# Layer 1's stick-breaking values and keys by two 1024-column units in a leading ordered list

## The chip, the cores and the metric

The kernel runs on one core of one Trainium2 chip. The metric is the device time of one execution in microseconds (us). The kernel before has a median of 2146.02 us over three runs (2145.95 to 2146.85). The core has five engines that matter here: PE (TensorE, the matmuls), DVE (VectorE), ACT (ScalarE), POOL (GpSimd) and SP (SyncE, which issues the loads). Each takes its instructions in the order in which the program wrote them.

## The reference

Two layers, each a hybrid of two kinds of attention beside each other, an output projection, and an MLP, all in float32 on x of 256 rows by 2048 columns:

```
for l in range(2):
    h = rms_norm(x, attn_norm)
    proj = h @ w_in                       # 2048 x 6160
    g_q, g_k, g_v, g_gate, g_lr, s_q, s_k, s_v = split(proj)
    o_gla = gla_chunked(g_q, g_k, g_v, log_sigmoid(g_lr @ w_gate_up + b_gate) / 16)
    o_gla = rms_norm(o_gla) * silu(g_gate)
    o_sb  = rms_norm(stick_breaking(rms_norm(s_q), rms_norm(s_k), s_v))
    x = x + concat(o_gla, o_sb) @ w_o
    x = x + square(relu(rms_norm(x) @ w_up)) @ w_down     # 8192 hidden
```

The columns of `proj` that this change touches are s_v (stick-breaking values, 1024 columns), s_k (keys, 1024 columns) and the first 512 columns of g_v (GLA values, 1024 columns) of the first layer.

## The kernel before, in words

**Precision.** Every large matmul is done as three: each float32 operand is split in a high part (rounded to the matmul's own format by an ACT copy, `whi`) and a low part (the remainder, a DVE subtraction, `wlo`), and the products high x high, high x low and low x high are summed in PSUM. A raw weight tile is loaded by SP, ACT writes its `whi`, DVE its `wlo`, PE reads both. For some tiles the low part is made without DVE: ACT writes the negated high part and a DMA issued by POOL adds the raw weights to it (`dlo`).

**Two kinds of code.** The attention part of a layer is written as *plain units*: `unit` computes all 256 rows by up to 512 columns from all 2048 inputs in four groups of weights, two halves each, 12 matmuls of 512 columns per half, 96 in all (L577, L578, L579). Small work between the units is hung on ticks by `after(n, fn)`: it is issued n halves later. The rest of a layer (second half of the gate, output projection, MLP) is one *ordered list*: every step is entered in a `Plan` with an engine, a length and its dependences, PE, SP and POOL keep the order in which steps were entered, and for DVE and ACT the planner writes an order by due times, by playing the list through with its own lengths. The list starts with five PE pieces of 12 matmuls each that stand for the end of the plain unit before it.

**Units of the list.** A unit of 1024 columns takes its 2048 inputs in eight pairs of 128-row blocks. A pair is a 2 x 2 block product for rows and inputs, so eight products of three matmuls (24 matmuls of 512 columns). For the pairs in `FAST = (1, 3, 5, 6)` it is done with seven products (21 matmuls), Strassen's scheme: DVE first makes sums of the weights (`first` and two `vector` steps, L1092) and of the activations (`forms`: `sums` with four 128x128 subtractions, L436 to L439, `high` on ACT, L450, and `low` on DVE, L454). The pairs in `ADDED = (2, 7)` have their low parts by the POOL DMA (L1269, L1272). The units called `iv` and `ik` are s_v and s_k of the *next* layer, done so at the end of a layer's list. Their results are scaled by the row norms (`AF.Copy` with `st["rst"]`, L1464) and kept in `natural`.

**Order of the first layer.** x is loaded in four parts (xb), PE turns each (L469) and ACT and DVE make the high and low operand `hT` from it (L479, L485). The first plain unit, s_v columns 0 to 511, starts on the first part while the others arrive by hooks after its halves. The row norms `st["rst"]` need the sums of squares of all x: `norm_squares` on ACT (L511), hung on ticks 6 to 9, then `norm_finish`. After it: s_k 0 to 511, the unit of the gate's low-rank and first query columns (272 wide), 256 query columns, s_v 512 to 1023, s_k 512 to 1023, s_q, four transposed units for g_q and g_k, g_v 0 to 511, g_v 512 to 1023, the first half of the gate; then the layer's ordered list. The second layer has the same attention part without the four s_v and s_k units, which the first layer's list has done.

**Pools.** The attention's temporaries lie in a scope `att`, the list's in a scope `mlp`, which take each other's place in SBUF; PSUM is cut into two accumulators and four small tiles for the attention, and into eight single banks for a list. Activations rotate through 17 buffers (`act`).

Of the kernel before, what the change touches and what calls it, by code (L numbers as in the profile page):

```python
# [144 lines left out]
def trunk_kernel(  # L145
# [60 lines left out]
    ATT = ("wg", "ident16", "mask16", "tri", "nones", "gmask", "reset", "v4", "lr", "lrT", "ha", "hh", "hl", "hA", "on", "dec", "S", "kdz", "row", "bc")  # L206
# [24 lines left out]
    open_scope("sbuf", att=1)  # L231
# [99 lines left out]
    def load_small():  # L331
        load_gains(1, (
            ("sq", sb_q_norm, 1), ("sk", sb_k_norm, 1), ("mlp", mlp_norm, KT),
            ("gla", gla_out_norm, 1), ("so", sb_out_norm, 1),
        ))
        load_gate_up(0)
# [85 lines left out]
    def forms(op, i, t, tag):  # L422
# [35 lines left out]
    def operand_parts(op, n, h2, key, l, place):  # L458
# [30 lines left out]
        def scaled():  # L489
            t = tmp("t2", [P, 2, T], bufs=T2)  # L490
# [6 lines left out]
    def norm_operand(op, n, key, l, sums=False):  # L497
        for h2 in range(2):
            turn, high, low, scaled = operand_parts(op, n, h2, key, l, ps_tile)
            turn()  # L500
            if sums and fast(2 * n + h2):
                for part in forms(op, 2 * n + h2, scaled(), "sxh"):
                    part()
            else:
                high()
                low()
# [288 lines left out]
    hT = Operand()  # L795
    ssq = new_ssq()
    st = {}
    his = []
    load_gains(0, (("attn", attn_norm, KT),))
    load_x(0, parts=2)  # L800
    wait_on_x(WARM0)
    st["first"] = turn_gains(0)
    norm_operand(hT, 0, "attn", 0)
    wait_on_x(WARM1)

    for l in range(DEPTH):
        wl = w_in[l]
        mixed = Operand()
        nxt = {}

        if l == 0:
            hooks = {}

            def next_x(n):
                load_x(n)
                with tc.issue_after(st["mm"]):
                    norm_operand(hT, n, "attn", 0)

            for n, at in ((1, (0, 0)), (2, (0, 1)), (3, (1, 1))):
                hooks[at] = lambda n=n: next_x(n)  # L820

            def begin():
                st["rst"] = norm_finish(ssq)

            for n in range(4):
                after(6 + n, lambda n=n: norm_squares(n, ssq))
            after(10, begin)
            after(2, build_constants)
            after(7, load_small)
            after(11, finish_small)  # L830
            uv = unit(
                hT, wl, 0, C_SV, 512, hooks=hooks, fine=1,
                order=lambda i, k: his[4 * i + (3 if i else k)] if i or k else None,
            )
            v = tmp("v4", [P, NT, 512], bufs=2)
            after(3, lambda a=uv, b=v: values(a, b))
        else:
            open_scope("sbuf", att=1)
            att_psum()
            load_gate_up(l)  # L840
            after(2, build_constants)
            v = natural["iv"][0]

        def sb_heads(g, qT, kT, v, first):

            state = {}

            def scores(hp):
                state[hp] = sb_scores(qT, kT, 2 * hp)
                after(3, lambda: weights(hp))  # L850

            def weights(hp):
                state[hp] = sb_weights(*state[hp])
                after(1, lambda: outs(hp))

            def outs(hp):
                po = ps_tile()
                for j in range(2):
                    sb_out(po, j, state[hp], v, 2 * hp + j)
                o = norm_pair(po)  # L860
                after(3, lambda: to_operand(mixed, 4 + 2 * g + hp, o, gain("so", l)))

            for hp in range(2):
                after(first[hp], lambda hp=hp: scores(hp))


        if l == 0:
            uk = unit(hT, wl, 0, C_SK, 512)
            rst = st["rst"]
            kT = act_tile(F32)  # L870
            sb_qk(uk, 0, 4, 0, rst, None, kT, 4)
        else:
            rst = st["rst"]
            kT = act_tile(F32)
            sb_qk(None, 0, 4, 0, rst, None, kT, 3, natural["ik"][0])
        ua = unit(hT, wl, 0, C_LR, RANK + 2 * P)
        lr = tmp("lr", [P, NT, RANK], bufs=1)
        for tt in range(NT):
            nc.vector.tensor_scalar(
                lr[:, tt, :], ua[:, tt, :RANK], rst[:, tt : tt + 1], None, ALU.mult  # L880
            )
        qT = act_tile(F32)
        sb_qk(ua, RANK, 2, 0, rst, gqk[:, l : l + 1], qT, 5)


        gt = {}

        def gate_rows():
            lrT = tmp("lrT", [RANK + 1, T], bufs=1)
            nc.gpsimd.memset(lrT, 1.0)  # L890
            plr = ps_tile()
            for tt in range(NT):
                nc.tensor.transpose(plr[:RANK, tt * P : (tt + 1) * P], lr[:, tt, :], ident)
            nc.vector.tensor_copy(lrT[:RANK, :], plr[:RANK, :T])
            gt["row"] = row_of(rst)
            gt["lrT"] = lrT

        def gates(b):
            if b == 0:
                gt["e"] = [act_tile(F32) for _ in range(3)]  # L900
                gt["dec"] = tmp("dec", [P, 4, 4], bufs=1)
            eb, enb, ekd = gt["e"]
            pl = ps_tile()
            for e in range(2):
                ee = 2 * b + e
                nc.tensor.matmul(
                    pl[:, e * T : (e + 1) * T], kc["wg"][:, ee * P : (ee + 1) * P], gt["lrT"],
                    start=(e == 0), stop=True, skip_group_check=True,
                )
            a = tmp("t2", [P, 512], bufs=T2)  # L910
            nc.scalar.activation(a, pl, AF.Abs)
            nc.scalar.activation(a, a, AF.Exp, scale=-1.0)
            nc.scalar.activation(a, a, AF.Ln, bias=1.0)
            nc.vector.scalar_tensor_tensor(a, pl, 0.0, a, ALU.min, ALU.subtract)
            bc = tmp("t2", [P, 512], bufs=T2)
            for e in range(2):
                es = slice(e * T, (e + 1) * T)
                nc.vector.tensor_tensor_scan(
                    bc[:, es], kc["reset"], a[:, es], 0.0, ALU.mult, ALU.add
                )  # L920
            bs = slice(2 * b, 2 * b + 2)

# [790 lines left out]
```

## Time and profile before

| what | value |
|---|---|
| median of three runs | 2146.02 us |
| profiled execution, its own time | 2147.3 us |
| profiled execution, span from first to last instruction | 2145.6 us |
| PE busy | 2134.1 us, 99% of the span |
| DVE busy | 1892.2 us, 88% |
| ACT busy | 1474.0 us, 69% |
| POOL busy | 159.9 us, 7% |
| granted TensorE clock | 1.0 |
| HBM read | 405.12 MB |

How to read it: a row of a timeline has the start and the length in us, the engine, the line, the operation, what it writes from what it reads with its shape, how often it stands there in a row, and in brackets how long the engine had been idle and what ended that. Matmuls are pipelined, so the time that one costs in a dense stretch is the distance between two starts, not its length. "PEld" is the loading of the stationary operand, which overlaps.

### The profile page before, as it was taken

How to read it: one execution, taken by the hardware profiler on the slowest of the kernel's cores; microseconds unless marked ns; L12 is line 12 of the kernel's file. 1: busy time of each engine (PE TensorE's matmuls, PEld its weight loads, DVE VectorE, ACT ScalarE, POOL GpSimd, SP SyncE). 2: the span in 40 equal slices, each digit the busy share in tenths (PEclk: the TensorE clock that was granted, in tenths of full speed). 3: DMA queues.
4: the chain of work that ended last, by engine and by line, in shares of the span. 5: the costliest groups of instructions: out<-in, count | busy, mean ns of one | idle time of the engine just before them, and what ended most of it. 6: DMA issues, size and time to landing. Idle time of an engine off the chain costs nothing.

```text
span 2145.6 us, 28380 instructions
## 1 busy us (share of the span) xinstructions
PE 2134.1 (99%) x10232; PEld 1780.4 (83%) x10232; DVE 1892.2 (88%) x2533; ACT 1474.0 (69%) x1889; POOL 159.9 (7%) x210
## 2 busy tenths in 40 slices
PE   9999999999999999999999999999999999999999
PEld 7988888888888888888878888888888888888887
DVE  5677669999999999999998975799999999999998
ACT  5555356687677677678776654667876776776775
POOL 0020000000000000000001200000000000000000
PEclk9999999999999999999999999999999999999999
DMA  6655455688888878878886544657888888888886
GB/s 229 190 159 165 164 192 193 197 244 262 250 252 243 266 243 247 271 236 256 238 242 172 177 157 157 202 172 229 248 249 274 236 260 246 249 249 251 255 249 182
DMA packets 169105, 480.37 MB, mean 224 GB/s; under 512 B 9370, under 2 KB 34530, under 8 KB 168964
## 3 DMA queue, kind: packets, MB, share of 16 engines
q1 hardware_dynamic: 149380, 407.24, 55.3%
q0 software_dynamic: 19584, 71.31, 17.6%
q8 instruction: 80, 1.31, 0.2%
q14 instruction: 61, 0.50, 0.1%
HBM read 405.12 MB, written 2.10 MB: 190 GB/s over the span
## 4 chain that ended last, share of the span: by engine, by line
PE 93%; DVE 4%; DMA 1%; issue 1%; ACT 1%; SPq 0%; POOL 0%; DVEq 0%; ACTq 0%
PE acc L577 4%; PE acc L579 4%; PE acc L578 4%; PE acc L624 3%; PE acc L628 1%; DMA raw<-in_w_in_dram 1%; DVE wlo L1263 1%; DVE wlo L560 0%; DVE xb L1092 0%; PE ps L742 0%; PE ps L688 0%; PE ps L1060 0%; PE ps L706 0%; DVE t L645 0%; PE ps L1053 0%
## 5 line engine op out<-in xcount | busy, mean ns | idle before, releaser
L1259 ACT ACTIVATE whi<-raw 128x1024 fp32r<-128x1024 f32 (+1 forms) x768 | 739.9, 978 | 317.7 <-issue 45.1
L1263 DVE TENSOR_TENSOR wlo<-raw,whi 128x1024 fp32r<-128x1024 f32 (+1 forms) x632 | 690.4, 1099 | 65.0 <-ACT whi L1259 52.5
L560 DVE TENSOR_TENSOR wlo<-raw,whi 128x1024 fp32r<-128x1024 f32 (+2 forms) x162 | 181.3, 1123 | 100.0 <-ACT whi L558 99.8
L558 ACT ACTIVATE whi<-raw 128x1024 fp32r<-128x1024 f32 (+2 forms) x162 | 155.9, 968 | 158.2 <-PE acc L579 110.4
L1272 POOL DMA_DIRECT2D dlo<-raw x136 | 117.5, 865 | 1587.9 <-ACT dlo L1269 864.2
L1259 ACT ACTIVATE whi<-ts 128x1024 fp32r<-128x1024 f32 x144 | 152.8, 1061 | 72.7 <-DVE ts L1092 3.7
L577 PE MATMUL acc<-whi,act 128*128 128x512 f32 (+2 forms) x512 | 191.9, 375 | 1.0 <-ACT act L479 1.0
L578 PE MATMUL acc<-wlo,act 128*128 128x512 f32 (+2 forms) x512 | 187.2, 366 | 0.6 <-DVE wlo L560 0.6
L579 PE MATMUL acc<-whi,act 128*128 128x512 f32 (+2 forms) x512 | 187.2, 366 | 0.0
L1263 DVE TENSOR_TENSOR wlo<-ts,whi 128x1024 fp32r<-128x1024 f32 x144 | 175.9, 1222 | 10.7 <-ACT whi L1259 7.7
L1092 DVE TENSOR_TENSOR ts<-raw 128x1024 f32<-128x1024 f32 x144 | 175.9, 1222 | 1.6
L1269 ACT ACTIVATE dlo<-raw 128x1024 fp32r<-128x1024 f32 x136 | 139.3, 1046 | 3.6 <-PE m__1930_9313 L1373 1.7
L577 PEld LDWEIGHTS acc<-whi,act 128*128 128x128 f32 x512 | 97.1, 190 | 19.0 <-issue 3.0
L579 PEld LDWEIGHTS acc<-whi,act 128*128 128x128 f32 x512 | 96.8, 189 | 16.0 <-DVE act L485 0.2
L578 PEld LDWEIGHTS acc<-wlo,act 128*128 128x128 f32 x512 | 96.9, 189 | 14.7 <-DVE wlo L560 0.8
L1092 DVE TENSOR_TENSOR raw<-raw 128x512 f32<-128x512 f32 x144 | 99.3, 689 | 2.3
L1092 DVE TENSOR_TENSOR raw<-ts,raw 128x512 f32<-128x512 f32 x144 | 98.9, 686 | 0.5
L624 PE MATMUL acc<-act,whi 128*128 128x512 f32 x256 | 91.8, 401 | 0.0
L628 PE MATMUL acc<-act,wlo 128*128 128x256 f32 x256 | 71.6, 280 | 0.0
L1464 ACT ACTIVATE act<-act,st 128x512 f32<-128x512 f32 x72 | 49.2, 714 | 19.2 <-DVE act L1092 19.2
L454 DVE TENSOR_TENSOR act<-t,act 128x512 fp32r<-128x512 f32 x84 | 57.3, 686 | 0.0
L624 PEld LDWEIGHTS acc<-act,whi 128*128 128x128 f32 x256 | 48.1, 188 | 10.7
(3145 smaller groups left out, 5336.4 us busy)
## 6 DMA issues: line engine op xcount, KB each, us to landing
raw<-in_w_up_dram SPq DMA_DIRECT2D x112, 1024.0 KB, 5.4
raw<-in_w_down_dram SPq DMA_DIRECT2D x112, 1024.0 KB, 5.8
raw<-in_w_in_dram SPq DMA_DIRECT2D x82, 1024.0 KB, 5.1
dlo<-raw POOLq DMA_DIRECT2D x136, 512.0 KB, 6.5
raw<-in_w_o_dram SPq DMA_DIRECT2D x32, 1024.0 KB, 5.0
raw<-in_w_up_dram SPq DMA_DIRECT2D x32, 512.0 KB, 6.4
raw<-in_w_down_dram SPq DMA_DIRECT2D x32, 512.0 KB, 6.1
raw<-in_w_in_dram SPq DMA_DIRECT2D x18, 512.0 KB, 5.8
```

Source lines behind the costliest of these rows:

```text
L558: newest["hi"] = nc.scalar.activation(h, r, AF.Copy).ins
L560: newest["lo"] = nc.vector.tensor_tensor(lo[:, q : q + step, :width], r, f32(h), ALU.subtract).ins
L577: nc.tensor.matmul(o, xh[:, sl], whi[:, j, :width], start=first, stop=False)
L578: nc.tensor.matmul(o, xh[:, sl], wlo[:, j, :width], start=False, stop=False)
L579: st["mm"] = nc.tensor.matmul(o, xl[:, sl], whi[:, j, :width], start=False, stop=last).ins
L624: nc.tensor.matmul(acc[:, f, :], whi[:, j, sl], op.both(k), start=(k == 0), stop=False, skip_group_check=True,)
L628: nc.tensor.matmul(acc[:, f, T:], wlo[:, j, sl], xh, start=False, stop=(k == KT - 1), skip_group_check=True,)
L1092: nc.vector.tensor_tensor(dst, a, b, op)
L1259: nc.scalar.activation(box["h"][:, :n], src(), AF.Copy)
L1263: nc.vector.tensor_tensor(box["l"][:, :n], src(), f32(box["h"][:, :n]), ALU.subtract)
L1269: nc.scalar.activation(box["l"], src(), AF.Copy, scale=-1.0)
L1272: nc.gpsimd.dma_start(f32(box["l"]), src(), accum_op=ALU.add)
```

## The change

The first layer's s_v and s_k are now done by units `iv` and `ik` too, 1024 columns each, with the seven-product pairs. For that the list's code becomes a function `ordered(l, units, ...)`, called with l = -1 for a list of only these two units, and then once for each layer as before. Ahead of the short list stands one plain unit, as something to run while x arrives: g_v columns 0 to 511 of the first layer (`u0`), which before stood late in the attention part. So the first layer's attention part becomes the second layer's, less that one unit.

The parts, by name:

- `u0` computes g_v 0 to 511; its result is scaled into `natural["gv"]` by the short list's `copy_first`. The sums of squares are hung on ticks 5 to 8, and the norms' end (`norm_end([], ssq_first)`) is the first entry of the short list.
- `norm_operand` also keeps the turned float32 activations of the four fast pairs (`scaled(turned0[i])`, two ACT activations of 128x256 per pair, one tick later). From them the short list makes the sums' operands: `forms` for i in 1, 3, 5, 6, each four DVE subtractions of 128x128, one ACT copy and one DVE subtraction of 128x512. The plain high and low operands exist already and are not made again.
- The constants of the attention, the small gains and the gate's weights are built and loaded at the start of each layer's attention part (ticks 2 and 5), after the scope `att` is opened there.
- The three gate tiles of each layer's GLA move from `act` buffers to an own tag `eg` in `att`.
- In the first layer the first two GLA pairs are hung on ticks 4 and 7 of the one g_v unit left (the others stay on ticks 1 and 4 of the unit behind theirs).

In the built program PE has 24 matmuls fewer: four pairs in each of two units, three matmuls each.

```diff
-            todo.append((op.pair(i), t))
+            if i not in op.t:
+                todo.append((op.pair(i), t))
...
-    def norm_operand(op, n, key, l, sums=False):
+    def norm_operand(op, n, key, l):
         for h2 in range(2):
...
+            if fast(i):
+                k = FAST.index(i)
+                if k % 2 == 0:
+                    turned0["t"] = act_tile(F32, (P, 2, 2, T))
+                turned0[i] = turned0["t"][:, k % 2]
+                after(1, lambda scaled=scaled, i=i: scaled(turned0[i]))
...
+    def layer_units(l):
+        units = []
+        if l >= 0:
+            units = [("g", 0, 0), ("o", 0, 0), ("o", 0, 1)]
+            units += [(k, q, n2) for q in range(4) for k in ("up", "down") for n2 in range(2)]
+        if l + 1 < DEPTH:
+            units += [("iv", 0, 0), ("ik", 0, 0)]
+        return units
...
+    def ordered(l, units, hT, rst, ug, gates_t, mixed=None, ons=None):
...
+        if l < 0:
+            rst, rst_done = norm_end([], ssq_first)
+            st["rst"] = rst
         for tt in range(NT):
             gate_done[0, tt] = add(
-                "ACT", A1, lambda tt=tt: copy_first(tt), before[-2], gate_done.get((0, 0))
+                "ACT", A1, lambda tt=tt: copy_first(tt), before[-2], gate_done.get((0, 0)), rst_done
             )
...
+        if l < 0:
+            for i in FAST:
+                done["iv", 0, i] = made(
+                    lambda i=i: forms(hT, i, turned0[i], None), None, True, None
+                )
+        else:
+            hT = Operand()
+            gate(0)
...
+    for n in range(4):
+        after(5 + n, lambda n=n: norm_squares(n, ssq_first))
+    u0 = unit(
+        hT, w_in[0], 0, C_GV, 512, hooks=hooks, fine=1,
+        order=lambda i, k: his[4 * i + (3 if i else k)] if i or k else None,
+    )
+    natural["gv"] = act_tile(F32, (P, NT, 512))
+    ordered(-1, layer_units(-1), hT, None, u0, [natural["gv"]])
+
+    for l in range(DEPTH):
...
+        if l == 0:
+            load_small()
+            after(5, finish_small)
+        v = natural["iv"][0]
...
-                gt["e"] = [act_tile(F32) for _ in range(3)]
+                gt["e"] = [tmp("eg", [P, 4, T], bufs=3) for _ in range(3)]
...
-        if l == 0:
-            uv = unit(hT, wl, 0, C_SV + 512, 512)
-            v = values(uv, tmp("v4", [P, NT, 512], bufs=2))
-            uk = unit(hT, wl, 0, C_SK + 512, 512)
...
+            ready = l == 0 and g == 0
+            if ready:
+                v = natural["gv"]
+            else:
+                v = values(unit(hT, wl, 0, C_GV + g * 512, 512), tmp("v4", [P, NT, 512], bufs=2))
             for hp in range(2):
-                after(1 + 3 * hp, lambda e=2 * g + hp, v=v, c=hp * 2 * P: gla_pair(e, v, c))
+                after((4 if ready else 1) + 3 * hp, lambda e=2 * g + hp, v=v, c=hp * 2 * P: gla_pair(e, v, c))
```

More of the change, by code (lines that the diff above doesn't have):

```diff
@@ L495, in operand_parts @@
         return turn, high, low, scaled
-    def norm_operand(op, n, key, l, sums=False):
+    turned0 = {}
+    def norm_operand(op, n, key, l):
         for h2 in range(2):
+            i = 2 * n + h2
             turn, high, low, scaled = operand_parts(op, n, h2, key, l, ps_tile)
             turn()
[L501 to L506, printed above, removed]
+            high()
+            low()
+            if fast(i):
[4 more added lines that the diff above has]
+                after(1, lambda scaled=scaled, i=i: scaled(turned0[i]))
     def norm_squares(n, ssq):
```

488 lines of the change are left out of this document (229 added, 259 removed).

## The prediction

> **What bounds the kernel now.** I read the page first, then busy times by stage, then timelines of the start, where the change works.
>
> ```profile
> span 2145.6 us, 28380 instructions
> PE 2134.1 (99%) x10232; PEld 1780.4 (83%) x10232; DVE 1892.2 (88%) x2533; ACT 1474.0 (69%) x1889; POOL 159.9 (7%) x210
> 297.00:1077.00 780.00, 779.41 (x3535) 647.12 (x3534) 738.13 (x948) 582.53 (x719) 55.39 (x64) 1.00 0.80 242
> 1077.00:1163.90 86.90, 85.83 (x384) 70.20 (x383) 80.15 (x107) 64.00 (x86) 11.65 (x21) 1.00 0.77 214
> ```
>
> PE is busy for 99% of the span, so a removed matmul is worth its full distance and a new PE wait costs its full length. The two stretches (length, then busy us of PE, PEld, DVE, ACT, POOL, then clock, DMA share, GB/s) are layer 1's list up to and from its last two units, iv and ik. DVE is busy there 92 to 95%, yet PE hardly waits: a list runs without stalls once DVE and ACT are ahead. So the gain is read from PE's pitch, and the cost from the places where PE must wait for DVE to get ahead, above all the head of the new list.
>
> ```profile
> 33.76 0.39 PE L577 MATMUL acc<-whi,act 128*128 128x512 f32 x1
> ...
> 34.89 0.39 PE L579 MATMUL acc<-whi,act 128*128 128x512 f32 x1
> 35.12 0.39 PE L577 MATMUL acc<-whi,act 128*128 128x512 f32 x1
> ```
>
> These are the end of the first plain unit and the start of the next. Six starts from 33.76 to 35.12: 0.227 us per matmul of 512 columns. The unit ends at 35.12.
>
> **The change, part by part.**
>
> *Removed.* 24 matmuls x 0.227 = 5.44 us of PE, the whole of the gain.
>
> *First plain unit.* g_v 0 to 511 in place of s_v 0 to 511: same matmuls, same turns of x, so PE should end it at 35.12 again. ACT gets four pairs of `scaled` copies more, and two of its eight squares come earlier, into gaps:
>
> ```profile
> 23.97 1.57 ACT L479 ACTIVATE act<-ps,gcol_a 128x256 fp32r<-128x256 f32 x4 [2.88 <-PE ps L469]
> 25.41 2.02 ACT L558 ACTIVATE whi<-raw 128x1024 fp32r<-128x1024 f32 x2
> 27.31 0.64 ACT L511 ACTIVATE t<-xb 128x512 f32<-128x512 f32 x1
> ...
> 27.92 0.64 ACT L511 ACTIVATE t<-xb 128x512 f32<-128x512 f32 x1
> 1083.25 0.84 ACT L492 ACTIVATE t<-m__2009_9687,gcol_a 128x256 f32<-128x256 f32 x2
> 1083.96 0.64 ACT L511 ACTIVATE t<-xb 128x512 f32<-128x512 f32 x1
> ```
>
> At 23.97 ACT had been idle for 2.88 us, waiting for PE to turn x; the third pair's copies and the first squares (0.71 + 2 x 0.61 us) fit there. From 23.97 on ACT is full: high parts to 25.41; a weight copy (0.95), the last pair's scaled copies (0.71, the distance of the last two rows), a weight copy (0.95), six squares of 0.61. Sum: 31.7. Without those gaps the copies would push the high parts by some 2 us, which PE would not see: it needs the last ones only after 24 more matmuls (5.4 us).
>
> *The head of the new list.* In the changed order of instructions DVE has, behind the plain unit's last low part: the reduction of the squares, the mean, four groups of four subtractions with four low parts among them, three small steps of the norm, and only then the low part of the first weights that PE needs. ACT has its four high copies ahead of those weights' high part.
>
> ```profile
> 34.26 0.16 DVE L517 TENSOR_REDUCE st<-ssq 128x2 f32<-128x8 f32 x1 [1.04 <-ACT t L511]
> 34.46 0.17 DVE L382 TENSOR_SCALAR st<-st 128x2 f32<-128x2 f32 x1
> ...
> 37.56 0.15 DVE L389 TENSOR_TENSOR st<-st 128x2 f32<-128x2 f32 x1
> ...
> 37.94 0.16 DVE L391 SCALAR_TENSOR_TENSOR st<-st,st 128x2 f32<-128x2 f32 x1
> 1094.35 0.28 DVE L436 TENSOR_TENSOR t<-t 128x128 f32<-128x128 f32 x1
> 1094.55 0.28 DVE L437 TENSOR_TENSOR t<-t 128x128 f32<-128x128 f32 x1
> 1094.87 0.29 DVE L438 TENSOR_TENSOR t<-t,t 128x128 f32<-128x128 f32 x1
> 1095.19 0.29 DVE L439 TENSOR_TENSOR t<-t,t 128x128 f32<-128x128 f32 x1
> 1095.40 1.22 DVE L1263 TENSOR_TENSOR wlo<-raw,whi 128x1024 fp32r<-128x1024 f32 x1
> 1098.28 1.29 DVE L454 TENSOR_TENSOR act<-t,act 128x512 fp32r<-128x512 f32 x2
> 1099.48 1.22 DVE L1263 TENSOR_TENSOR wlo<-raw,whi 128x1024 fp32r<-128x1024 f32 x1
> ```
>
> A group of four subtractions takes 1.05 us (1094.35 to 1095.40), two low parts of an operand 1.20 (1098.28 to 1099.48), a small step 0.2. DVE's queue holds still until ACT's last square at 31.7. Then 0.3 for reduction and mean, 4 x 1.05 = 4.2, 4 x 0.6 = 2.4, 3 x 0.2 = 0.6: the first weights' low part starts at 39.2 to 39.3 and ends 1.22 later, at 40.5. (ACT: the fourth group is done at 32.0 + 4.2 + 1.2 = 37.4, its high copy at 38.0, the weights' high part at 39.1: not last.) PE does one matmul with the high part alone, 0.23 us, and then needs the low part. It ended the unit at 35.12, so it loses 40.5 - 35.35 = 5.2 us. The planner's five pieces of PE at the list's head stand for 13.6 us of cover; here there is 35.1 - 31.7 = 3.4.
>
> The same place in layer 1's list shows what such a head costs where DVE is ahead:
>
> ```profile
> 298.00 0.50 PE L1373 MATMUL m__536_2766<-wlo,act 128*128 128x512 f32 x1 [0.59 <-DVE wlo L1263]
> ```
>
> 0.59 us: with no more than that here, the change would gain (first rival).
>
> *Behind the head.* DVE's next eight pieces (low parts and weight sums of the first fast pair: five at a distance of 1.13, two of 0.6, the last 1.22 long, and 0.3 of short waits for ACT) end at 40.4 + 8.4 = 48.8; PE needs the last of them, for the pair's third step, at 40.5 + 36 x 0.227 = 48.7. I take 0.2 us with the hand-over. Then comes pair 2, whose low part is made by ACT and the POOL DMA.
>
> ```profile
> 1104.75 1.99 ACT L1269 ACTIVATE dlo<-raw 128x1024 fp32r<-128x1024 f32 x2
> L1272 POOL DMA_DIRECT2D dlo<-raw x136: 852/862/1018, 404.7 to 2126.5; - x136
> DMA to landing us min/median/max: 4.5/6.5/11.8
> dlo<-raw POOLq DMA_DIRECT2D x2, 512.0 KB, 10.2
> ```
>
> The ACT copy (1.0 us) stands behind the copy of the first pair's sums, which are ready at 43.2; so it ends at 45.3, and a landing of 6.5 us puts the low part at 51.85. PE needs it at 48.9 + 6 x 0.227 = 50.2. Bounds: 4.5 us lands at 49.85, no wait; 10.2, the median of the run's first two such DMAs, at 55.5, 5.3 us. I take the median of all, 1.6 us, as nearest: by SP's order one load ends beside it and the next begins later. The Trainium skill ("DMA: Bandwidth & Descriptors", section "Anatomy of one DMA — SWDGE (gpsimd) path") fits 2.0 us and bytes over 436e3; for 512 KB that is an estimate of 3.2 us, no wait, and the sum would be 1.6 us lower. The trace's fastest is 4.5, so the page does not hold for these adding DMAs, and the sum goes by the rows.
>
> *The rest of the list* I cost at nothing: its DVE work is that of iv and ik above less the operand forms and layer tail, which PE ran through with 1.1 us idle in 86.9. If that cover fails, those 1.1 us.
>
> *Attention of layer 1.* It becomes layer 2's, so its price is the difference of the two in this trace.
>
> ```profile
> 57.30 0.28 PE L577 MATMUL acc<-whi,act 128*128 128x272 f32 x1
> 297.03 0.39 PE L1372 MATMUL m__536_2766<-whi,act 128*128 128x512 f32 x1
> 1163.95 0.28 PE L577 MATMUL acc<-whi,act 128*128 128x272 f32 x1
> ...
> 1361.55 0.39 PE L1372 MATMUL m__2553_12337<-whi,act 128*128 128x512 f32 x1
> 1167.83 0.40 PE L578 MATMUL acc<-wlo,act 128*128 128x272 f32 x1 [0.59 <-DVE wlo L560]
> 1209.96 0.30 PE L688 MATMUL ps<-ident,act 128*128 128x128 f32 x1 [0.92 <-DVE act L651]
> ```
>
> Layer 2: 1361.55 - 1163.95 = 197.6. Layer 1: 297.03 - 57.30 = 239.73, less two s units inside (192 x 0.227 = 43.55) is 196.18. So 1.4 us more, which the last two rows explain: PE waits 0.59 us for weights behind ik's tail on DVE and 0.92 for normalised keys, because no plain unit covers them. Between 0 (if they are layer 2's own) and 2.4 (if the two GLA pairs, now five ticks earlier, close behind the keys' turns, add another wait of that size); I take 1.4.
>
> *Moved at no cost.* Constants on POOL, small gains and gate weights go behind SP's first three loads of layer 1's attention, as layer 2 has its own there.
>
> ```profile
> 29.37 0.31 SPq L307 DMA_DIRECT2D t<-in_sb_q_norm_dram  x1
> ```
>
> Five small loads more, 0.3 us each, hold SP some 1.6 us before the fourth weights, which PE wants only after three groups. If that cover fails, at most those 1.6. The gate tiles leave the activations' ring, which loosens it; g_v takes one buffer of it.
>
> *Sum.* -5.44 + 5.2 + 0.2 + 1.6 + 1.4 = +3.0 us on the span of 2145.6; that execution took 2147.3, 1.3 above the median of the runs, so I put the difference on the median: 2146.02 + 3.0 = 2149.0. The limit of what tells a change of this kernel is 0.2%, 4.3 us: no change that can be told.
>
> **The rivals.**
>
> *DVE and ACT are ahead after all.* If PE meets the list as in the row at 298.00 (0.6 us): -5.44 + 0.6 + 1.4 = -3.4, 2142.6; with no price in the attention 2141.2. It decides for "faster" where head, dlo wait and attention together stay under 1.15 us. For it: lists elsewhere start so. Against: the squares end at 31.7 and 7.5 us of DVE work lie between.
>
> *The adding DMA lands late.* Its first use may be slow, as those two of 10.2 us. Then the wait is 5.3 in place of 1.6: +6.7, 2152.7. It turns the verdict to "slower" from a landing of 7.8 us on (1.3 us longer than the median, 4.3 in all). Against: the median of 136 is 6.5, and little loads beside it.
>
> *PE's clock falls in the gap.*
>
> ```profile
> PE ps L527 <- POOL ident masks.py:199: 1.6, 1, 1.6
> ...
> 8.63 0.79 PE L577 MATMUL acc<-whi,act 128*128 128x512 f32 x1 [1.04 <-ACT act L479]
> ...
> 12.24 0.57 PE L579 MATMUL acc<-whi,act 128*128 128x512 f32 x1
> 12.65 0.39 PE L577 MATMUL acc<-whi,act 128*128 128x512 f32 x1
> ```
>
> At the kernel's start nine matmuls go at 0.43 us, 8.63 to 12.45, then at 0.227. The longest wait of PE in the trace, the first of these rows, is 1.6 us, before it has done anything; the new gap is 4 us, one matmul, then 1.2. If the slow state returns for as long, 9 x 0.2 = 1.8 us, all of which hide in the two waits behind the head (0.2 + 1.6): still +3.0, 2149.0. If it lasts twice that, +4.8, 2150.8. The Trainium skill ("TensorE: Matmul & The Clock Gate", section "What's actually happening") says that the clock halves after an idle window of about 3.4 us and returns after as long of work; the windows run freely, so a gap of 4 us may or may not hold one. The start agrees with the second half (3.8 us); no row here shows the first.
>
> *DVE stays the bound for the whole list.* Against: 80.15 us of DVE in 86.9 with more work; a start at 31.7 ends well before PE's 40.5 + 81.6. I leave it in the rest.
>
> **How the numbers follow.** Forecast 0.45 (0.38 within 0.2%, 0.07 above, where attention or head run over); clock 0.2 (0.09 within, 0.11 slower); late DMA 0.2, slower; DVE ahead 0.1 (0.07 faster, 0.03 within); rest 0.05, slower. So faster 0.07, same 0.50, slower 0.43. The range leaves out the first rival's 0.1 and a tail above of about as much: below, no dlo wait, no attention price and a head of 4.9 give -0.7, and a little more, 2145.0; above, the late DMA, 2152.8.
>
> **What would show it.** PE idle from 35.1 for about 4 us (released by ACT's `whi`), then about 1.2 (by DVE's `wlo`); DVE idle before the reduction to about 31.7; PE's third wait by a `dlo` near 50; 10208 matmuls; first attention part without g_v as long as the second without it. It is wrong if ACT ends the squares earlier or DVE's subtractions run faster on x than in the row, if the dlo lands outside 4.5 to 10, or if the first ticks of attention wait for small loads.

## The result and the profile after

The changed kernel takes 2152.82 us (median of nine runs, 2151.24 to 2154.09) where the kernel before, beside it, takes 2146.65 (nine runs, 2145.67 to 2147.66): a ratio of 1.0026, with a 95% interval of 1.0017 to 1.0034. It is slower by about a quarter of a per cent, although it has 24 matmuls fewer. On the median of 2146.02 from which the prediction counted, the ratio gives 2151.6 us; forecast were 2149.0. The profiled execution took 2152.86 us, its span is 5.6 us longer than before.

The page after, span and busy times:

```profile
span 2151.2 us, 28506 instructions
PE 2131.0 (99%) x10208; PEld 1777.2 (83%) x10208; DVE 1934.1 (90%) x2601; ACT 1499.5 (70%) x1927; POOL 167.5 (8%) x218
```

10208 matmuls are there, PE is busy for 3.1 us less, and the span is longer: what was added is waiting, and products at half speed, which count as busy. Where PE waited up to 380 us, by the waits of the trace (what waited, for what; us in total, times, longest):

```profile
PE m__86_455 L1107 <- ACT whi L994: 4.0, 1, 4.0
PE m__606_2943 L1107 <- ACT act L867: 2.4, 1, 2.4
PE ps L692 <- DVE act L655: 2.1, 3, 1.0
PE m__86_455 L1108 <- DVE wlo L998: 0.5, 1, 0.5
```

The first and the last are the head of the new list, which the prediction had. The third is the wait for normalised keys in layer 1's attention, which it had too. The second, at the head of layer 1's own list, is in no term of it. PE's timeline after, at the two heads and at the stage borders:

```profile
33.72 0.39 PE L583 MATMUL acc<-whi,act 128*128 128x512 f32 x1
38.14 0.80 PE L1107 MATMUL m__86_455<-whi,act 128*128 128x512 f32 x1 [4.03 <-ACT whi L994]
39.40 0.80 PE L1108 MATMUL m__86_455<-wlo,act 128*128 128x512 f32 x1 [0.46 <-DVE wlo L998]
39.99 0.63 PE L1109 MATMUL m__86_455<-whi,act 128*128 128x512 f32 x1
...
42.98 0.56 PE L1107 MATMUL m__87_456<-whi,act 128*128 128x512 f32 x1
43.38 0.39 PE L1108 MATMUL m__87_456<-wlo,act 128*128 128x512 f32 x1
...
122.72 0.28 PE L581 MATMUL acc<-whi,act 128*128 128x272 f32 x1
298.52 0.39 PE L583 MATMUL acc<-whi,act 128*128 128x512 f32 x1
301.27 0.50 PE L1107 MATMUL m__606_2943<-whi,act 128*128 128x512 f32 x1 [2.36 <-ACT act L867]
...
302.79 0.63 PE L1107 MATMUL m__607_2944<-whi,act 128*128 128x512 f32 x1
303.21 0.63 PE L1108 MATMUL m__607_2944<-wlo,act 128*128 128x512 f32 x1
...
305.77 0.57 PE L1108 MATMUL m__606_2943<-wlo,act 128*128 128x512 f32 x1
306.19 0.40 PE L1109 MATMUL m__606_2943<-whi,act 128*128 128x512 f32 x1
```

At 0.227 us per matmul the first unit ends at 33.95. PE stands until 38.14, does one matmul, stands again until 39.40: 4.19 + 1.03 = 5.2 us. From 39.40 to 43.38 the products go at 0.43 us, half speed, as at the kernel's start: 1.9 us more. The new list takes 122.72 - 38.14 = 84.58 us; 360 matmuls x 0.2268 are 81.65, and the rest of 2.9 is those 1.03 and 1.9, so nothing else waits in it. At 298.75 PE stands for 2.52 us more, where before it lost 0.75 (297.03 to 298.00 in the prediction's rows, less one matmul), and again eight products go at half speed, 1.6 us.

DVE's timeline ahead of the head:

```profile
30.69 0.16 DVE L881 TENSOR_REDUCE st<-ssq 128x2 f32<-128x8 f32 x1 [2.44 <-ACT t L515]
30.96 0.28 DVE L434 TENSOR_TENSOR t<-act 128x128 f32<-128x128 f32 x1
...
37.45 0.69 DVE L453 TENSOR_TENSOR act<-t,act 128x512 fp32r<-128x512 f32 x1
38.12 1.23 DVE L998 TENSOR_TENSOR wlo<-raw,whi 128x1024 fp32r<-128x1024 f32 x1
```

The reduction waits 2.44 us for ACT's last square; the subtractions and low parts take from 30.96 to 38.1; only then comes the first low part of a weight. The sum of the stretches, before against after: -5.4 (24 products), -1.2 (the first unit starts 0.4 earlier and loses 0.8 less at the start), -0.4 (PE's turn of the small gains, L316, which stood in the second plain unit of before and now stands in layer 1's attention), +5.2 and +1.9 (new list's head), +1.6 (layer 1's attention: 298.75 - 122.72 = 176.03, before 196.18 less one unit of 21.77), +1.8 and +1.6 (head of layer 1's list), +0.5 (all of layer 2). That is +5.6, the difference of the spans. The -1.2 is no effect of the change: the same first plain unit ends between 32.90 and 35.71 us in the profiles of the changed kernel and its variants below, so the start alone differs by up to 2.8 us between profiles.

### The profile page after: what moved, and what is told of

Its sections match the earlier page's. It is cut to its first block, busy times and chain, and to the rows that moved or that the text cites. A ratio compares the mean times of both kernels' runs of the same rounds, so it can differ in the third digit from the quotient of the medians.

```text
span 2151.2 us, 28506 instructions
## 1 busy us (share of the span) xinstructions
PE 2131.0 (99%) x10208; PEld 1777.2 (83%) x10208; DVE 1934.1 (90%) x2601; ACT 1499.5 (70%) x1927; POOL 167.5 (8%) x218
## 4 chain that ended last, share of the span: by engine, by line
PE 94%; DVE 4%; ACT 1%; issue 1%; DMA 1%; SPq 0%; POOL 0%; DVEq 0%; ACTq 0%
PE acc L628 3%; PE acc L581 3%; PE acc L582 2%; PE acc L583 2%; PE acc L632 1%; DMA raw<-in_w_in_dram 1%; DVE wlo L564 1%; DVE wlo L998 0%; PE ps L746 0%; PE ps L1663 0%; DVE t L649 0%; DVE st L650 0%; PE ps L692 0%; DVE act L827 0%; PE ps L1656 0%
## 5 line engine op out<-in xcount | busy, mean ns | idle before, releaser
L994 ACT ACTIVATE whi<-raw 128x1024 fp32r<-128x1024 f32 (+1 forms) x808 | 777.3, 976 | 338.6 <-issue 48.2
L998 DVE TENSOR_TENSOR wlo<-raw,whi 128x1024 fp32r<-128x1024 f32 (+1 forms) x664 | 725.2, 1099 | 74.8 <-ACT whi L994 60.0
L562 ACT ACTIVATE whi<-raw 128x1024 fp32r<-128x1024 f32 (+2 forms) x130 | 122.0, 944 | 112.7 <-PE acc L583 67.0
L564 DVE TENSOR_TENSOR wlo<-raw,whi 128x1024 fp32r<-128x1024 f32 (+2 forms) x130 | 141.6, 1092 | 62.3 <-ACT whi L562 62.1
L827 DVE TENSOR_TENSOR ts<-raw 128x1024 f32<-128x1024 f32 x152 | 185.8, 1222 | 1.7
L581 PE MATMUL acc<-whi,act 128*128 128x512 f32 (+2 forms) x384 | 140.9, 367 | 0.3 <-ACT act L478 0.3
L582 PE MATMUL acc<-wlo,act 128*128 128x512 f32 (+2 forms) x384 | 136.9, 356 | 0.9 <-DVE wlo L564 0.9
L583 PE MATMUL acc<-whi,act 128*128 128x512 f32 (+2 forms) x384 | 136.7, 356 | 0.0
L581 PEld LDWEIGHTS acc<-whi,act 128*128 128x128 f32 x384 | 72.6, 189 | 13.6 <-issue 2.5
L582 PEld LDWEIGHTS acc<-wlo,act 128*128 128x128 f32 x384 | 72.6, 189 | 10.5 <-DVE wlo L564 1.6
L583 PEld LDWEIGHTS acc<-whi,act 128*128 128x128 f32 x384 | 72.4, 189 | 10.6 <-DVE act L484 0.2
L449 ACT ACTIVATE act<-t 128x512 fp32r<-128x512 f32 x88 | 54.4, 622 | 3.6 <-DVE t L437 3.5
```

What stands on the lines that cost most here:

```text
L562: newest["hi"] = nc.scalar.activation(h, r, AF.Copy).ins
L564: newest["lo"] = nc.vector.tensor_tensor(lo[:, q : q + step, :width], r, f32(h), ALU.subtract).ins
L581: nc.tensor.matmul(o, xh[:, sl], whi[:, j, :width], start=first, stop=False)
L582: nc.tensor.matmul(o, xh[:, sl], wlo[:, j, :width], start=False, stop=False)
L583: st["mm"] = nc.tensor.matmul(o, xl[:, sl], whi[:, j, :width], start=False, stop=last).ins
L827: nc.vector.tensor_tensor(dst, a, b, op)
```

## The experiments

Each kernel ran beside the kernel before on the same chip, and ratios are to that.

**The head of layer 1's list: which bank lies under what.** The attention's two accumulators and the list's eight banks share the same PSUM. Layer 1 had 14 plain units and has 9 now; layer 2 has 10. With an odd count the last one, the gate unit, has the other accumulator. My theory was that banks 1 and 6, into which the list's first products go, now lie under the gate unit's own sums, so that PE must wait until ACT has copied them out (L867). The first run hands the banks out in another order in layer 1:

```diff
-                mlp_psum()
+                mlp_psum((5, 7, 1, 6, 2, 4, 3, 8) if l == 0 else (1, 6, 5, 7, 2, 4, 3, 8))
```

> The changed kernel, with one thing more: in layer 1 alone the mlp half's eight banks are handed out in the order 5, 7, 1, 6 in place of 1, 6, 5, 7, so that the gate unit's accumulator, which after the change is the other buffer of its pool, lies again under banks that the first products of layer 1's own list don't write. All of the computation stays. Theory A (the pair of banks): the 2.5 us in which TensorE waits at the head of layer 1's list for ScalarE's copies of the gate unit's sums falls to about the 0.75 us of the kernel before, the eight products at 0.43 us behind it run at 0.227 us, and the time falls by 2.5 to 3.5 us against the changed kernel, to about 2149.5 us beside a kernel before at 2146.6, a ratio of 1.0013. Rival B (the first weights or ScalarE are late there for another reason, such as its backlog from the new attention stage): the wait stays within 0.3 us and ends with another tile, and the ratio stays at 1.0026.

Measured: 2150.82 us (11 runs, 2148.79 to 2152.09), ratio 1.0015 (1.0006 to 1.0024), so 2.0 us by the medians and 2.4 by the ratios below the changed kernel, a little less than expected. PE's timeline of this run:

```profile
299.90 0.39 PE L583 MATMUL acc<-whi,act 128*128 128x512 f32 x1
300.12 0.39 PE L1107 MATMUL m__608_2945<-whi,act 128*128 128x512 f32 x1
301.05 0.50 PE L1108 MATMUL m__608_2945<-wlo,act 128*128 128x512 f32 x1 [0.53 <-DVE wlo L998]
```

The wait for ACT's copies is gone, one of 0.53 us for a low part is there as in the kernel before, and no product behind it is slow. The counter-test makes the same swap in the kernel before, where the count is even:

> The kernel before, with layer 1's banks handed out in the order 5, 7, 1, 6 in place of 1, 6, 5, 7 and nothing else, so that here, where the gate unit has the other accumulator, the banks of the first products of layer 1's own list lie under that accumulator. All of the computation stays. Theory A (the pair of banks is the whole cause of the wait at that head): the wait grows from 0.6 us to 2.4 us and ends with ScalarE's copies of the gate unit's sums, up to eight products behind it run at 0.43 us, and the time grows by 1.8 to 3.4 us, a ratio of 1.0008 to 1.0016. Rival B (the wait came with the change's own work, so with ScalarE's or VectorE's backlog): the wait stays at 0.6 us and the ratio is 1.0000.

Measured: 2149.33 us against 2146.63, ratio 1.0014 (1.0005 to 1.0022). PE's timeline of this run:

```profile
298.44 0.80 PE L1372 MATMUL m__538_2768<-whi,act 128*128 128x512 f32 x1 [2.36 <-ACT act L1137]
299.03 0.63 PE L1373 MATMUL m__538_2768<-wlo,act 128*128 128x512 f32 x1
...
301.17 0.62 PE L1372 MATMUL m__539_2769<-whi,act 128*128 128x512 f32 x1
```

The same 2.36 us and the same slow products, in a kernel without any of the change's work. The pairing of accumulator and banks is the cause; the change only flipped it by changing the number of plain units.

**The head of the new list.** The sums for the seven products were put behind pair 0's weights. The edit gives them the end of the plain unit (the last of the planner's five pieces for it) as their earliest place; in the profile with both mends they then start at 36.82, behind both low parts of pair 0:

```diff
-                    lambda i=i: forms(hT, i, turned0[i], None), None, True, None
+                    lambda i=i: forms(hT, i, turned0[i], None), None, True, before[-1]
```

> The changed kernel, with the subtractions that form half the pairs' sums and low parts for seven products put behind the last piece of pair 0's weights in the planner's order (their earliest place was the start). All of the computation stays. Theory A (the prediction's term: VectorE does 16 subtractions, 4 low parts and the norm's steps ahead of the new list's first low part of a weight): the wait at the head of the new list falls from 5.2 us to 0.6 us or less, the eight products at 0.43 us go with it (1.8 us), and the time falls by 5 to 7 us against the changed kernel, to a ratio of about 0.9997 to the kernel before. Rival B (VectorE has too much to do in this stretch whatever its order): the wait moves to the first product of pair 1, which wants the sums, by the 16 subtractions' 16 x 0.4 = 6 us, and the ratio stays within 0.0005 of 1.0026.

Measured: 2150.24 us (2147.43 to 2151.42), ratio 1.0016 (1.0007 to 1.0025), so 2 to 3 us gained where 5 to 7 were expected. With the banks mended too:

> The changed kernel with both edits: layer 1's banks in the other order, and the sums for seven products behind pair 0's weights. All of the computation stays. If the two heads of the lists are all that the change costs beyond its 24 products less (-5.4 us), and they add up, the time is that of the kernel before - 5.4 + 1.4 (layer 1's attention) + 0.5 to 1, so 3 to 4 us below it: a ratio of 0.9981 to 0.9986. The rival, that a cost not yet seen sits elsewhere, gives a ratio of 0.9995 or more although both waits are gone.

Measured: 2146.13 us (2144.86 to 2147.51), ratio 0.9998 (0.9989 to 1.0007). The rival held: both waits are gone, and the gain isn't there. PE's and DVE's timelines of the run with both:

```profile
33.80 0.39 PE L1107 MATMUL m__78_423<-whi,act 128*128 128x512 f32 x1
34.03 0.39 PE L1108 MATMUL m__78_423<-wlo,act 128*128 128x512 f32 x1
...
40.28 0.50 PE L1108 MATMUL m__78_423<-wlo,act 128*128 128x512 f32 x1 [0.30 <-DVE wlo L998]
42.62 0.51 PE L1108 MATMUL m__76_421<-wlo,act 128*128 128x512 f32 x1 [0.68 <-DVE wlo L998]
44.82 0.50 PE L1108 MATMUL m__74_419<-wlo,act 128*128 128x512 f32 x1 [0.53 <-DVE wlo L998]
```

```profile
35.67 1.23 DVE L998 TENSOR_TENSOR wlo<-raw,whi 128x1024 fp32r<-128x1024 f32 x1 [2.09 <-ACT whi L994]
36.82 0.28 DVE L434 TENSOR_TENSOR t<-act 128x128 f32<-128x128 f32 x1
...
37.87 1.22 DVE L827 TENSOR_TENSOR ts<-raw 128x1024 f32<-128x1024 f32 x1
```

PE goes from the unit into the list without a gap. But the list now takes 85.45 us, 3.8 over its matmuls, most of it in short waits for low parts between 36 and 45 us: the subtractions that no longer stand ahead of pair 0 stand among pair 1's low parts. Part of the wait moved. DVE had been idle ahead of that twice, 2.44 us for ACT's squares (as after) and 2.09 for a high part that stands behind ACT's first copy of the first unit's sums.

**The clock in the gap.** The run fills the gap with 17 matmuls into a spare tile:

```diff
+    pw = ps_tile()
+    for _ in range(17):
+        nc.tensor.matmul(pw, hT.parts(0)[0][:, :P], hT.both(0), start=True, stop=True)
     natural["gv"] = act_tile(F32, (P, NT, 512))
```

> The changed kernel, with 17 matmuls more between the first plain unit and the new list, 512 wide and all into one spare tile that nobody reads (17 x 0.227 = 3.9 us, so that they fit into the wait of 4.2 us there and leave the waits themselves as they are). It does work that the reference doesn't ask for. Theory A (the granted clock falls because TensorE stands idle for some 4 us and takes some 3.4 us of work to come back): the eight products at 0.43 us behind the wait run at 0.227 us, and the time falls by about 1.6 to 1.8 us against the changed kernel, to a ratio of about 1.0018. Rival B (the clock falls for another reason, or the slower products are hidden by the next wait): no change, ratio 1.0026 or a little above.

Measured: 2151.27 us (2149.31 to 2151.68), ratio 1.0019 (1.0010 to 1.0028), as theory A had it, though the interval overlaps that of the changed kernel. The timeline shows it directly:

```profile
34.99 4.01 PE L1445 MATMUL ps<-act 128*128 128x512 f32 x17
39.18 0.50 PE L1107 MATMUL m__87_473<-whi,act 128*128 128x512 f32 x1 [0.18 <-ACT whi L994]
40.44 0.51 PE L1108 MATMUL m__87_473<-wlo,act 128*128 128x512 f32 x1 [0.76 <-DVE wlo L998]
40.78 0.39 PE L1109 MATMUL m__87_473<-whi,act 128*128 128x512 f32 x1
41.01 0.39 PE L1107 MATMUL m__87_473<-whi,act 128*128 128x512 f32 x1
```

The wait itself stays, the products behind it start 0.227 us apart, and the new list takes 83.02 us in place of 84.58. The second filling used transposes (the helper issues so many transposes of the identity):

```diff
+    wait_on_x(36)
     natural["gv"] = act_tile(F32, (P, NT, 512))
```

> The changed kernel, with 36 transposes of the identity more between the first plain unit and the new list (128 wide, about 0.11 us each, 3.9 us in all, into a spare tile that nobody reads), in the place where another run had 17 matmuls, which kept the clock at full speed through the wait. It does work that the reference doesn't ask for. Theory A (for the clock, transposes are work like matmuls): no product at 0.43 us at the head of the new list, and a ratio of about 1.0019 as with the matmuls. Rival B (the clock counts multiplications alone; the Trainium skill's page TensorE: Matmul & The Clock Gate states in its Part 4 that transposes don't count as work): about 8 products at 0.43 us as in the changed kernel without the filling, and a ratio of about 1.0026.

PE's timeline of this run, and two stretches of 3.41 us in it (length, then busy us of PE, PEld, DVE, ACT, POOL, then clock, DMA share, GB/s), the second of which follows the first:

```profile
34.15 4.09 PE L531 MATMUL ps<-ident 128*128 128x128 f32 x36
38.35 0.50 PE L1107 MATMUL m__87_492<-whi,act 128*128 128x512 f32 x1
39.61 0.51 PE L1108 MATMUL m__87_492<-wlo,act 128*128 128x512 f32 x1 [0.76 <-DVE wlo L998]
39.95 0.39 PE L1109 MATMUL m__87_492<-whi,act 128*128 128x512 f32 x1
40.18 0.39 PE L1107 MATMUL m__87_492<-whi,act 128*128 128x512 f32 x1
35.38:38.79 3.41, 3.31 (x28) 2.81 (x26) 3.27 (x11) 2.38 (x5) 0.00 (x0) 1.00 0.00 0
38.79:42.21 3.42, 2.66 (x12) 2.18 (x12) 3.13 (x4) 2.55 (x4) 0.00 (x0) 1.00 0.08 7
```

In this profile transposes held the clock as matmuls did. In the first of the two stretches PE did transposes and, from 38.35 on, less than 0.5 us of products; by the rule found in the last section, the second stretch would have gone at half clock if transposes didn't count as work. The Trainium skill ("TensorE: Matmul & The Clock Gate", section "Part 4: PE-mode transpose") says that a transpose doesn't count as PE-busy in the same way; this trace doesn't agree, though it is one profile, and its rows don't show whether these float32 transposes of the identity are the mode that the page means. The times don't decide it: 2154.64 us in the median of five runs that lie 6 us apart (2152.34 to 2158.26), ratio 1.0042 (1.0029 to 1.0056). Why this kernel is slower and scatters so stays open.

**What is left of the change when its heads are mended.** The price in layer 1's attention was tested by moving the turns of the keys (on top of both mends):

```diff
-        sb_qk(None, 0, 4, 0, rst, None, kT, 3, natural["ik"][0])
+        sb_qk(None, 0, 4, 0, rst, None, kT, 6, natural["ik"][0])
...
-        sb_qk(None, 0, 4, 0, rst, None, kT, 5, natural["ik"][1])
+        sb_qk(None, 0, 4, 0, rst, None, kT, 9, natural["ik"][1])
```

> The changed kernel with both mends (layer 1's banks in the other order, the sums behind pair 0's weights), and with the turns of the stick-breaking keys queued some steps later in the plain units of both layers (6 in place of 3, 9 in place of 5). All of the computation stays. Theory A (TensorE waits for the normalised keys, 2.1 us and 0.4 us beside it in layer 1 and about 1.5 us in layer 2, because their turns come too early, and VectorE has them done a few steps later anyway): these waits go, and the time is 2.5 to 4 us below that with the two mends alone, a ratio to the kernel before of 0.9980 to 0.9988. Rival B (the scores that want the keys then wait in place of the turns): the ratio stays within 0.0005 of 0.9998.

Measured: 2144.03 us against 2146.63, ratio 0.9988 (0.9979 to 0.9997), at the edge of theory A's band; by the medians it is 2.1 us below the run with both mends, where 2.5 to 4 were expected. The waits for keys are gone from the profile, and two others of 0.3 us came up in each layer. In the profiles, from the start of layer 1's attention to that of its list, it takes 174.3 us where the run with both mends takes 176.0. Then the backlog of DVE was taken on: the sums of the first two pairs go ahead of the norm's reduction, into DVE's idle time, those of the others stay behind pair 0's weights:

```diff
+        if l < 0:
+            for i in FAST[:2]:
+                done["iv", 0, i] = made(lambda i=i: forms(hT, i, turned0[i], None), None, True, None)
         rr = rr_done = rst_done = None
         if l < 0:
             rst, rst_done = norm_end([], ssq_first)
...
-            for i in FAST:
+            for i in FAST[2:]:
```

> As the run before in this row (both mends, the keys' turns later), but the sums of the first two of the four pairs for seven products are put ahead of the norm's reduction on VectorE, which stands idle there for 2.4 us until ScalarE has its last squares, and only the other two pairs' behind pair 0's weights. All of the computation stays. Theory A (what is left of the waits in the new list, 2.5 us with the two mends, is VectorE's backlog of these subtractions): the waits for low parts of weights between 37 us and 46 us fall to 1 us or less, and the time falls by 1.5 to 2.5 us beside the run before. Rival B (ScalarE, which is held by its two copies of the first unit's sums and now has two high copies more ahead of the first weights, sets these waits): the waits stay or a new one appears at the head of the list, and the time stays within 0.5 us.

Measured: 2142.58 us (2140.25 to 2144.90) against 2146.63, ratio 0.9977 (0.9968 to 0.9986): the first that is more than 0.2% below the kernel before. DVE's and PE's timelines:

```profile
27.20 0.29 DVE L434 TENSOR_TENSOR t<-act 128x128 f32<-128x128 f32 x1
...
30.77 0.15 DVE L881 TENSOR_REDUCE st<-ssq 128x2 f32<-128x8 f32 x1
```

```profile
33.87 0.50 PE L1113 MATMUL m__82_439<-wlo,act 128*128 128x512 f32 x1 [0.58 <-DVE wlo L1003]
42.85 0.50 PE L1113 MATMUL m__78_435<-wlo,act 128*128 128x512 f32 x1 [0.53 <-DVE wlo L1003]
```

The eight subtractions now run from 27.20, in the gap ahead of the reduction. That starts 2.1 us ahead of the unit's end (30.77, the unit ends at 32.90), where it was 3.3 after the change (30.69 and 33.95), and a wait of 0.58 us is back at the head of the list, a part of what rival B expected. Two waits are left, and the new list takes 83.56 us where it took 85.43 in the run before: 1.9 us, as theory A had it, though the medians differ by only 1.45. Two last runs part what is due to which:

> The changed kernel with the mends of the two lists' heads alone: layer 1's banks in the other order, the sums of the first two pairs for seven products ahead of the norm's reduction, those of the other two behind pair 0's weights. The keys' turns stay where the change has them. All of the computation stays. Theory A (the gain of the change is its 24 products less, 5.4 us, and its own price, once the heads are mended, is 1.4 us in layer 1's attention and some 1.5 to 2 us of waits left in the new list): a time 1.5 to 2.5 us below the kernel before, a ratio of 0.9988 to 0.9993. Rival B (the gain of the fastest kernel so far is the keys' later turns, which have nothing to do with the change): a ratio of 0.9997 to 1.0003.

> The kernel before with the stick-breaking keys' turns queued later (6 in place of 3, 9 in place of 5), where only layer 2 has them. All of the computation stays. Theory A (the 1.1 us in which TensorE waits in layer 2 for normalised keys go): a time 0.5 to 1.2 us below the kernel before, a ratio of 0.9995 to 0.9998, so within what a measurement tells, with the two waits gone from the profile. Rival B (as much is lost where the scores want the keys): the waits move and the ratio is 1.0000.

Measured: with the heads mended and the keys left, 2145.39 us against 2146.06, ratio 0.9994 (0.9985 to 1.0003), which lies between the two theories' bands, with an interval that reaches into both; in the kernel before with the keys later, 2146.39, ratio 1.0000 (0.9991 to 1.0009). There the waits for keys are gone, layer 2's attention is 0.7 us shorter (196.92 in place of 197.60), and the time doesn't tell it. So the keys' later turns give little in the kernel before, because only layer 2 needs them there; they pay in the changed kernel, whose layer 1 has such waits too: its attention takes 176.0 us with the heads mended and 174.2 with the keys later as well. The change, both heads, the split of the sums and the keys together make the gain of 0.23%; every step short of that stays within 0.2%.

## Why the prediction was right and wrong

*Removed, -5.44.* Right: the new list without its waits takes 360 products at 0.2268 us.

*The head of the new list, 5.2.* Right in size and cause: 4.19 + 1.03 us, released by `whi` and then by `wlo`. The squares ended at 30.5 instead of 31.7, the low part started at 38.1 instead of 39.2, and the unit ended as much earlier (33.95 instead of 35.12), so the difference held; it is 4.18 us, too, in the run with the banks mended, whose unit ended at 35.71. That the subtractions' place in DVE's queue makes this wait is shown by the run that moved them: PE enters the list without a gap. What the prediction didn't say is that the work, once moved, comes back as most of 3.8 us of waits further down; the queue was short of time, not only badly ordered.

*Behind the head, 0.2 and 1.6.* Neither was seen in the profile after. The DMA's row there:

```profile
dlo<-raw POOLq DMA_DIRECT2D x2, 512.0 KB, 5.6
```

The first two adding DMAs, in the window from 40 to 60 us, landed in 4.7 and 6.4 us (the row has their median), and not the 6.5 or the 10.2 of the kernel before; POOL issued the first at 44.4, 0.9 us earlier than I had it, and the slow products let PE come to the low part only at 50.87. Where the clock stayed up (17 matmuls in the gap), the third step lost the 0.2, and no `dlo` was waited for; with transposes it was 0.4. The term of 1.6 was too large; the trace before, with 4.5 to 11.8, couldn't say so.

*The clock in the gap.* The rival came true, in its shorter form: nine products at half speed behind the gap cost 1.9 us, but the waits that were to hide it (0.2 + 1.6) were not there. So the prediction's arithmetic for "it hides" failed, though the sum of this place (1.8 for the waits, 1.9 for the clock) is the same: two misses of one size that cancel, which is luck. The prediction's sentence of the Trainium skill ("TensorE: Matmul & The Clock Gate", section "What's actually happening") has the clock halve after an idle window of about 3.4 us and come back after as long of work. The trace agrees with the second half: the clock is full again at 43.33, behind a stretch of 3.41 us in which PE was never idle. It doesn't agree with the first: the clock fell at 36.50, when PE had been idle for 2.4 us of the stretch of 3.41 (last section). The 3.8 us that the prediction read at the kernel's start are no measure of it either, for in the changed kernel's profile only two products are slow there.

*Attention of layer 1, 1.4.* Right in size, 1.6, and half right in its parts: PE waits for normalised keys, as the row at 1209.96 had shown for layer 2, but for 2.1 us in all; the wait of 0.59 us for weights, the prediction's other part, stays in layer 2 and doesn't come up in layer 1. Moving the keys' turns takes 1.7 us off this stage.

*The rest of the list, and what was moved, at nothing.* The rest of the new list is right: nothing more than 0.1 us is left of it. What failed is the tail of this step: I costed everything outside the parts touched at nothing, and layer 1's own list has a new wait at its head. The removal of five plain units flipped which accumulator the gate unit has, and with it which banks are free when the list begins: 1.8 us of wait and 1.6 of clock. These 3.4 us are more than the 2.6 by which the span lies above the forecast (+5.6 against +3.0); the easier start (-1.2, which is scatter) and smaller differences (-0.4, +0.2, +0.5, +0.1) make up the rest. The rows to see it were there: the gate unit's copies and the order of banks in the code, and the row at 298.00 with only 0.59, which I used as the picture of a healthy head and took for granted in the kernel after.

*The other rivals.* DVE was not ahead at the new list's head, no adding DMA landed late, and DVE didn't bind the whole list: PE runs through it from 43.4 us on without a wait.

So the sign and most of the size stand on the right step, the head of the new list, and "no change that can be told" missed by the flipped accumulator. That the range (2145.0 to 2152.8) holds the 2151.6 is partly luck: its upper end was the late adding DMA, which didn't come, and the room was filled by 3.4 us that no term had. The lower end has a slip: -5.44 + 4.9 is -0.5, or -0.3 with the 0.2 of the third step, not -0.7.

## What to carry to other kernels

When a change adds or removes uses of a rotating buffer, count the turns modulo the number of buffers up to the next place where that memory is handed to something else: a wait can appear in a stage that the change never touches. When work is put at the head of a dense stretch, ask what each in-order engine has ahead of the first item that the bottleneck needs, and whether it stood idle before; moving the work behind that item only helps if the queue has time for it later. A gap on PE costs more than its length, for the products behind it may run at half speed; whether they do also depends on where the gap falls, which the program doesn't set.

## What the hardware showed

A wait of 2.5 us was enough to halve the clock: in the profiles with that wait at the head of layer 1's list, eight products went at 0.43 us after the change, with the transposes, and (seven) in the kernel before with the banks swapped, while with pair 0's weights first and with the 17 matmuls none did. The slow stretch began within 1.5 us of the wait's end or at once.

The clock column of the traces says when. It changes only at the borders of stretches of 3.41 us (the two slow times of the changed kernel run from 36.50 to 43.33 and from 302.74 to 306.16: two such stretches and one, with 76 between them), and these borders lie elsewhere in each profile. Rows of stretches, in columns as above: four of the changed kernel, then two of the run with pair 0's weights first, which has the same wait of 2.36 us at the head of layer 1's list:

```profile
33.09:36.50 3.41, 1.02 (x5) 0.52 (x3) 3.27 (x12) 1.26 (x2) 0.00 (x0) 1.00 0.12 47
36.50:39.92 3.42, 1.32 (x2) 0.79 (x3) 3.05 (x7) 3.41 (x5) 0.00 (x0) 0.50 0.00 0
299.33:302.74 3.41, 1.47 (x6) 1.24 (x7) 2.16 (x3) 3.38 (x6) 0.00 (x0) 1.00 0.01 2
302.74:306.16 3.42, 3.42 (x9) 2.63 (x8) 2.54 (x3) 3.35 (x5) 0.00 (x0) 0.50 0.94 293
294.15:297.56 3.41, 1.59 (x8) 0.97 (x6) 1.34 (x3) 2.78 (x4) 0.00 (x0) 1.00 0.42 157
297.56:300.98 3.42, 2.88 (x13) 2.38 (x14) 2.49 (x3) 3.36 (x6) 0.00 (x0) 1.00 0.29 61
```

With the twelve traces of this case cut into such stretches, the clock is halved behind every one in which PE was busy for 1.47 us or less and behind none in which it was busy for 1.54 us or more. The wait of 2.36 us fell mostly into one stretch in the changed kernel and was split by a border (1.82 and 0.54) with pair 0's weights first. The Trainium skill ("TensorE: Matmul & The Clock Gate", section "What's actually happening") speaks of an idle window of about 3.4 us that runs freely; the length and the free running agree with these traces, but a wait of 2.5 can't hold a window, so a window needn't be idle throughout.

The mean granted clock of each execution bears it out beyond the profiles. Of the eleven executions of the run with pair 0's weights first, the three fastest (2147.43 to 2148.12 us) have a clock of 1.0 and the other eight (2148.57 to 2151.42) of 0.999; all nine of the changed kernel have 0.997 to 0.999, and all eleven with both mends 1.0.
